# A hybrid decoder layer: one group of forms for the query and key blocks, a later turn of the rotary tables, later angles for the attention, and a later start of five sums

## Chip, cores and metric

The kernel runs on one core of a Trainium2 chip. The metric is device microseconds of one execution. Engines are named as in the profile: PE is TensorE (matmuls), DVE is VectorE, ACT is ScalarE, POOL is GpSimd, SP is SyncE, which here only issues transfers.

## What is computed

One decoder layer on 256 tokens of 2048 features, in float32: a half feed-forward block, then two token mixers side by side (retention and sliding-window attention), then a second half feed-forward block and a gated embedding, with a layer norm after each. Cut to what matters here:

```
h = layer_norm(alpha * h + 0.5 * swiglu(h, w_ffn1_gu, w_ffn1_down), ...)
rq, rk, rv, rg, aq, ak, av, gate_r, gate_a = split(h @ w_in)
rq = rotary(rq as 8 heads of 128, positions, 128, 10000.0)
rk = rotary(rk as 8 heads of 128, positions, 128, 10000.0) * 128 ** -0.5
ro = head_group_norm(retention_chunkwise(rq, rk, rv as 8 heads of 256))
ret_branch = (silu(rg) * ro) @ w_ret_out
aq, ak = rotary(..., 16 of 64 features, 500000.0)
att_branch = sliding_window_attention_sinks(aq, ak, av, att_sinks) @ w_att_out
h = layer_norm(alpha * h + (sigmoid(gate_r) * ret_branch + sigmoid(gate_a) * att_branch) @ w_mix_out, ...)
h = layer_norm(alpha * h + 0.5 * swiglu(h, w_ffn2_gu, w_ffn2_down), ...)
```

The change lies in the mixers: in what is made for `rq`, `rk` and the rotary tables, and in sums of weights of the second feed-forward block that are made ahead during the mixers.

## The kernel before

**Precision and chunks.** A float32 product is made from two reduced-precision parts: a matrix x becomes hi (x rounded, made by an ACT cast) and lo (x minus hi, made by a DVE subtraction), and PE adds three products, lo·hi, hi·hi and hi·lo (L510 to L512). Weights come in chunks of 128 x 1024 floats (512 KB): SP issues the load into a raw tile (names that begin with r), ACT casts it to the hi tile (h, L162) and DVE makes the lo tile (l, L164). One chunk feeds 12 matmuls of 512 columns. So each chunk costs one ACT cast and one DVE subtraction, and PE's program is a row of chunks.

**Sevens.** In some blocks two chunks are worked off by a scheme with seven products instead of eight. It needs sums of weights (tiles u, v and b) and four sums of the activations, called forms. `forms_step(g, step)` makes those of the feature group g: step 0 adds hi and lo to full values (`whole`, tile gaf, L612) and makes the four sums (`forms_sums`, tile sums, L588 to L591), step 1 casts and subtracts (`forms_split`, tiles gafh and gafl). A unit p of a block reads the forms of group p // 2. The query and key blocks (`QK_UNITS`, tiles named rq and rk) use sevens for p = 0 and p = 1.

**Order.** It is written out by hand. The Python program emits for each chunk of PE the making of a chunk about four further on, then the chunk's matmuls, then one step of side work (`run_side`): one entry of the list `side`, one step of the first generator in `slow`, and one of the first in `lazy`. Each engine works its own instructions off in that order and waits where it needs another's result.

**The stage of the change**, in order of PE's time: two blocks of values side by side (tiles rv, 16 chunks), the query block rq, the key block rk, two more blocks of values (rv, eight chunks each), four gate blocks of eight chunks (tiles rg), a block av of four chunks, and then the attention's own products (aqk). What stands beside them:

- `rotary_table("r")` and `rotary_table("a")` make cosines and sines for the retention (tiles posr, rotr, trigr) and for the attention (posa, rota, triga). They are steps of one generator, `angles`, in `slow`. The first step issues the load of the positions on ACT's queue (L990). The second converts them and makes first angles (L993 to L1003), the third to sixth hold the seven rows of the reduction (L1006), then come, a step each, L1010, a sine on ACT (L1012), L1014 to L1018, and a second sine on ACT (L1020).
- `wide_tables` turns the finished retention table by four PE transposes (L1378, tile rtab) and ACT copies it out (L1382, tiles rtabc and rtabs).
- The side jobs of the queries and keys multiply by the wide tables (L1393, L1398, L1401), copy for the transposing transfer (ACT L227, tile wrk), issue it (SP L231, tile mrk), and join its result (ACT L238, tile rk1t).
- The retention of head h: PE makes scores (L1476, tile rs), DVE weighs them with the decay (L1480, L1481, tile rsc), one step later ACT and DVE split them (L113, L114, tile rsp), and one step after that PE multiplies them with the values (L1501, tile ro). Then DVE takes the statistics (L1508, L1509), a Newton root in small operations, and normalizes (L1522). For each pair of heads DVE multiplies by the gate (L1530, tile ron), ACT copies (L227, tile wro), SP issues a transposing transfer (tile mro), ACT joins it (L238), and ACT and DVE make the parts of the result (L1549, L1550, tile rett).
- `sums_ahead(items, wait, every)` in `lazy` makes the sums of weights of ten pairs of chunks of the second feed-forward block and stores them in DRAM. It loads its first pair, lets `wait` steps pass, and then works in four parts with `every` steps between them: two additions (L372, L373, tile u), a cast and two additions (L375 to L377, tile v), a cast and a subtraction (L379, L382, tile lu), a subtraction (L384, tile lv), with the stores (L386, L389) on SP.

Of the kernel before, what the change touches and what calls it, by code (L numbers as in the profile page):

```python
# [70 lines left out]
def layer(ctx: ExitStack, tc: tile.TileContext, io):  # L71
# [281 lines left out]
    def sums_ahead(items, wait, every):  # L353


        def pause():
            for _ in range(every):
                yield

        pairs = [[Chunk(k) for k in items[0]]]  # L360
        for _ in range(wait):
            yield
        for j, (key, _) in enumerate(items):
            a, b = pairs.pop()
            b11, b21, b12, b22 = a.of(a.raw, 0), a.of(a.raw, 1), b.of(b.raw, 0), b.of(b.raw, 1)
            u, v = (slot([P, 2, 512], F32, w + a.name) for w in "uv")
            t1, t3, t2, t4 = (x.rearrange("p (g n) -> p g n", g=2) for x in (u[:, 0], u[:, 1], v[:, 0], v[:, 1]))
            parts = [slot([P, 2, 512], F32R, w + a.name) for w in ("hu", "lu", "hv", "lv")]
            uh, ul, vh, vl = parts
            away = [dram.tile([P, 2, 512], F32, name=f"{w}{a.name}") for w in ("hud", "lud", "hvd", "lvd")]  # L370
            put_by_sums[key] = away
            dve.tensor_tensor(t1, b11, b12, ALU.add)  # L372
            dve.tensor_tensor(t3, b12, b22, ALU.add)  # L373
            yield from pause()
            act.copy(uh, u)  # L375
            dve.tensor_tensor(t2, b11, t3, ALU.add)
            dve.tensor_tensor(t4, t2, b21, ALU.add)  # L377
            yield from pause()
            act.copy(vh, v)  # L379
            if j + 1 < len(items):  # L380
                pairs.append([Chunk(k) for k in items[j + 1]])
            dve.tensor_tensor(ul, u, uh, ALU.subtract)  # L382
            yield from pause()
            dve.tensor_tensor(vl, v, vh, ALU.subtract)  # L384
            for e in range(2):
                sync.dma_start(away[e], parts[e].bitcast(F32))  # L386
            yield from pause()
            for e in range(2, 4):
                sync.dma_start(away[e], parts[e].bitcast(F32))  # L389
# [596 lines left out]
    def rotary_table(nm):  # L986

        inv, sgn = (0, 2) if nm == "r" else (1, 3)
        pos_i = slot([P, S], I32, "pos_i" + nm)
        act.dma_start(pos_i, io["positions"].broadcast_to([P, S]))  # L990
        pos = slot([P, S], F32, "pos" + nm)
        yield
        dve.tensor_copy(pos, pos_i)  # L993
        table = slot([P, 2, S], F32, "trig" + nm)
        cos, sin = trig[nm] = table[:, 0, :], table[:, 1, :]
        w = slot([P, 4, S], F32, "rot" + nm)
        ang, n, na, nb = (w[:, j, :] for j in range(4))
        dve.tensor_scalar(ang, pos, cst[:, inv : inv + 1], None, ALU.mult)
        dve.tensor_scalar(n, ang, INV_2PI, MAGIC, ALU.mult, ALU.add)
        dve.tensor_scalar(n, n, MAGIC, None, ALU.subtract)  # L1000
        dve.tensor_scalar(na, n, 1.0 / 2048.0, MAGIC, ALU.mult, ALU.add)
        dve.tensor_scalar(na, na, MAGIC, 2048.0, ALU.subtract, ALU.mult)
        dve.tensor_tensor(nb, n, na, ALU.subtract)  # L1003
        yield
        for who, j in ((na, 0), (nb, 0), (na, 1), (nb, 1), (na, 2), (nb, 2), (na, 3)):
            dve.scalar_tensor_tensor(ang, who, -TWO_PI[j], ang, ALU.mult, ALU.add)  # L1006
            if who is nb:
                yield
        yield
        dve.tensor_scalar(n, ang, 3.1415925, -3.1415925, ALU.min, ALU.max)  # L1010
        yield
        act.activation(nb, n, AF.Sin)  # L1012
        yield
        dve.tensor_scalar(sin, nb, cst[:, sgn : sgn + 1], None, ALU.mult)  # L1014
        dve.tensor_scalar(na, ang, 1.5707963267948966, None, ALU.add)
        dve.tensor_scalar(n, na, 3.141592653589793, -6.283185307179586, ALU.is_gt, ALU.mult)
        dve.tensor_tensor(na, na, n, ALU.add)
        dve.tensor_scalar(na, na, 3.1415925, -3.1415925, ALU.min, ALU.max)  # L1018
        yield
        act.activation(cos, na, AF.Sin)  # L1020
        yield
# [321 lines left out]
    def mixers(ht, norm, residual, keepers, away):  # L1343
# [29 lines left out]
        def wide_tables():  # L1373
            cos, sin = trig["r"]
            ps = bank("rtab").rearrange("p (w t n) -> p w t n", w=2, t=2)
            for j, v in enumerate((cos, sin)):
                for t in range(2):
                    pe.transpose(ps[:, j, t], v[:, t * P : t * P + P], ident)  # L1378
# [51 lines left out]

        def angles():
            yield from rotary_table("r")
            wide_tables()
            yield
            while len(rk) < 2:
                yield
            yield from rotary_table("a")

        slow.append(angles())
        for p in range(FRONT_PAIRS, KD // 2):  # L1440
            for n in range(2):
# [8 lines left out]
        slots_for_weights(14)  # L1450
        ahead = [(gu_keys("f2", j)(0, p), gu_keys("f2", j)(1, p)) for j in AHEAD for p in AHEAD[j]]
        lazy.append(sums_ahead(ahead[:2], 3, 3))
        lazy.append(sums_ahead(ahead[2:7], 2, 2))
        for b in range(2):
            got = mixer_block("rqk"[0] + "qk"[b], QK_UNITS[b], qk_keys(b), rhs)
            jobs = [rotated(v, f"r{'qk'[b]}{n}", (rq, rk)[b]) for n, v in enumerate(got)]
            assert not side
            side.extend(jobs[0][:3] + [jobs[0][3], jobs[1][0], jobs[0][4], jobs[1][1], jobs[1][2], jobs[1][3], jobs[1][4], jobs[0][6], idle, jobs[1][6]])
        made.clear()
        grp = 8  # L1460
        decay = [slot([P, 2, 384], F32, f"dec{j}") for j in range(4)]
# [648 lines left out]
```

## Time and profile before

| what | us |
|---|---|
| median of 3 runs | 2237.03 (2236.41 to 2239.07) |
| the profiled execution, own time | 2234.48 |
| the profiled execution, span | 2232.6 |
| stretch 750 to 820 of the span (queries and keys), by 10 us: DVE busy | 98 to 100% |
| stretches 820 to 830 and 830 to 840 | 83% and 70% |
| stretch 860 to 870: DVE busy | 57% |
| stretch 900 to 910: DVE busy | 99.6% |
| the same stretch: ACT busy, DMA engines busy | 79%, 75% |

The times of rows in the timeline count from the start of the span. A row gives the start, the time the instruction took, the engine, the line, the operation, its output and inputs, its size and, in brackets, how long the engine stood idle before it and what ended that. The time from the start of one matmul to the start of the next is shorter than what a row gives for it, since matmuls overlap; so costs on PE are read from starts. The same holds for DVE, where the next row starts some 0.08 us before the one ahead of it is noted as ended.

### The profile page before, as it was taken

How to read it: one execution, taken by the hardware profiler on the slowest of the kernel's cores; microseconds unless marked ns; L12 is line 12 of the kernel's file. 1: busy time of each engine (PE TensorE's matmuls, PEld its weight loads, DVE VectorE, ACT ScalarE, POOL GpSimd, SP SyncE). 2: the span in 40 equal slices, each digit the busy share in tenths (PEclk: the TensorE clock that was granted, in tenths of full speed). 3: DMA queues.
4: the chain of work that ended last, by engine and by line, in shares of the span. 5: the costliest groups of instructions: out<-in, count | busy, mean ns of one | idle time of the engine just before them, and what ended most of it. 6: DMA issues, size and time to landing. Idle time of an engine off the chain costs nothing.

```text
span 2232.6 us, 28924 instructions
## 1 busy us (share of the span) xinstructions
PE 2213.7 (99%) x9980; PEld 1827.5 (82%) x9980; DVE 2032.5 (91%) x2666; ACT 1475.6 (66%) x1707; POOL 48.4 (2%) x62
## 2 busy tenths in 40 slices
PE   9999999999999999999999999999999999999998
PEld 8888888888888787888788888888888878888877
DVE  6999999999988998989999888779999999899877
ACT  6877778777564656557866567457767678765553
POOL 0000000000000000000000000000000000000000
PEclk9999999999999999999999999999999999999999
DMA  9979889976687689866986578887899899777771
GB/s 314 274 227 267 248 245 264 246 241 232 231 291 243 234 273 352 277 228 222 286 247 208 185 210 324 321 301 256 294 306 314 290 264 270 218 238 240 279 289 70
DMA packets 315754, 576.00 MB, mean 258 GB/s; under 512 B 107084, under 2 KB 112076, under 8 KB 315608
## 3 DMA queue, kind: packets, MB, share of 16 engines
q1 hardware_dynamic: 305992, 543.79, 73.0%
q0 software_dynamic: 7632, 27.79, 6.6%
q10 hardware_dynamic: 1984, 2.58, 0.3%
q8 instruction: 78, 1.28, 0.2%
q14 instruction: 68, 0.56, 0.1%
HBM read 490.20 MB, written 33.55 MB: 235 GB/s over the span
## 4 chain that ended last, share of the span: by engine, by line
PE 89%; DVE 4%; DMA 4%; ACT 2%; issue 1%; SPq 0%; ACTq 0%; POOL 0%; DVEq 0%; POOLq 0%
PE f2g L512 2%; PE f2g L511 2%; PE f2g L510 2%; PE f1g L510 2%; PE f1g L512 2%; PE f1g L511 2%; PE f2u L512 2%; PE f1u L512 2%; PE f1u L510 2%; PE f1u L511 2%; PE f2u L511 2%; PE f2u L510 2%; PE aqk L461 2%; DMA rf_gu<-in_f_gu 2%; PE f2d L512 1%; PE f1e L511 1%
## 5 line engine op out<-in xcount | busy, mean ns | idle before, releaser
L164 DVE TENSOR_TENSOR lw_in_f<-rw_in_f,hw_in_f 128x1024 fp32r<-128x1024 f32 x124 | 148.7, 1219 | 17.3 <-ACT hw_in_f L162 17.2
L164 DVE TENSOR_TENSOR lf_gu<-rf_gu,hf_gu 128x1024 fp32r<-128x1024 f32 x123 | 145.5, 1222 | 18.6 <-ACT hf_gu L162 17.7
L162 ACT CAST hf_gu<-rf_gu 128x1024 fp32r<-128x1024 f32 x123 | 123.6, 1049 | 26.3 <-DMA rf_gu<-in_f_gu 25.0
L293 ACT CAST hvf_gu<-vf_gu 128x1024 fp32r<-128x1024 f32 x83 | 87.5, 1054 | 76.2 <-DVE vf_gu L289 64.7
L284 ACT CAST huf_gu<-uf_gu 128x1024 fp32r<-128x1024 f32 x83 | 87.3, 1051 | 75.9 <-DVE uf_gu L280 67.7
L164 DVE TENSOR_TENSOR lf_down<-rf_down,hf_down 128x1024 fp32r<-128x1024 f32 x96 | 115.8, 1221 | 22.1 <-ACT hf_down L162 17.4
L162 ACT CAST hw_in_f<-rw_in_f 128x1024 fp32r<-128x1024 f32 x124 | 125.4, 1048 | 6.1 <-DMA rw_in_f<-in_w_in_f 3.9
L162 ACT CAST hf_down<-rf_down 128x1024 fp32r<-128x1024 f32 x96 | 98.4, 1049 | 28.6 <-DMA rf_down<-in_f_down 13.5
L298 DVE TENSOR_TENSOR lvf_gu<-vf_gu,hvf_gu 128x1024 fp32r<-128x1024 f32 x83 | 101.4, 1222 | 0.0
L296 DVE TENSOR_TENSOR luf_gu<-uf_gu,huf_gu 128x1024 fp32r<-128x1024 f32 x83 | 101.4, 1221 | 0.0
L287 DVE TENSOR_TENSOR lf_gu<-rf_gu,hf_gu 128x1024 fp32r<-128x1024 f32 x83 | 101.4, 1221 | 0.0
L277 ACT CAST hf_gu<-rf_gu 128x1024 fp32r<-128x1024 f32 x83 | 86.8, 1046 | 9.5 <-DMA rf_gu<-in_f_gu 9.4
L510 PE MATMUL f1g<-hf_gu,xt 128*128 128x512 f32 x223 | 87.2, 391 | 0.0
L511 PE MATMUL f1g<-hf_gu,xt 128*128 128x512 f32 x223 | 87.0, 390 | 0.0
L512 PE MATMUL f1g<-lf_gu,xt 128*128 128x512 f32 x223 | 87.0, 390 | 0.0
L510 PE MATMUL f2g<-hf_gu,ht 128*128 128x512 f32 x196 | 76.4, 390 | 0.0
L512 PE MATMUL f2g<-lf_gu,ht 128*128 128x512 f32 x196 | 76.3, 389 | 0.0
L511 PE MATMUL f2g<-hf_gu,ht 128*128 128x512 f32 x196 | 76.2, 389 | 0.0
L510 PE MATMUL f1u<-hf_gu,xt 128*128 128x512 f32 x180 | 70.0, 389 | 0.0
L511 PE MATMUL f1u<-hf_gu,xt 128*128 128x512 f32 x180 | 70.0, 389 | 0.0
L512 PE MATMUL f1u<-lf_gu,xt 128*128 128x512 f32 x180 | 70.0, 389 | 0.0
L182 POOL DMA_DIRECT2D lf_gu<-rf_gu x37 | 32.2, 871 | 1641.5 <-DMA rf_gu<-in_f_gu 1134.4
(1640 smaller groups left out, 7331.3 us busy)
## 6 DMA issues: line engine op xcount, KB each, us to landing
rf_gu<-in_f_gu SPq DMA_DIRECT2D x362, 512.0 KB
rf_down<-in_f_down SPq DMA_DIRECT2D x176, 512.0 KB
rw_in_f<-in_w_in_f SPq DMA_DIRECT2D x148, 512.0 KB
lf_gu<-rf_gu POOLq DMA_DIRECT2D x37, 512.0 KB, 8.6
rw_rv<-in_w_rv SPq DMA_DIRECT2D x32, 512.0 KB
rw_ret<-in_w_ret SPq DMA_DIRECT2D x32, 512.0 KB
rw_mix<-in_w_mix SPq DMA_DIRECT2D x32, 512.0 KB
rw_pg<-in_w_pg SPq DMA_DIRECT2D x32, 512.0 KB
```

Of the source, the lines that this page charges most:

```text
L162: act.copy(c.hi, c.raw)
L164: dve.tensor_tensor(c.lo, c.raw, c.hi, ALU.subtract)
L277: act.copy(a.hi, a.raw)
L284: act.copy(uh, u)
L287: dve.tensor_tensor(a.lo, a.raw, a.hi, ALU.subtract)
L293: act.copy(vh, v)
L296: dve.tensor_tensor(ul, u, uh, ALU.subtract)
L298: dve.tensor_tensor(vl, v, vh, ALU.subtract)
L461: pe.matmul(ps[f], hi[:, kk, f * P : (f + 1) * P], rhs(k), start=k == 0, stop=k == n_k - 1,)
L510: pe.matmul(o, al, bh, start=first, stop=False)
L511: pe.matmul(o, ah, bh, start=False, stop=False)
L512: pe.matmul(o, ah, bl, start=False, stop=self.left == 0)
```

## The change

Four edits. The forms of the values' second half: group 1 is made no longer, and group 0 is made one unit later (p = 5 instead of 4). `wide_tables` runs two steps later. The attention's table begins eleven steps after the second key tile is joined, instead of at once; that join itself comes one step later, by a second idle step in the side list. The second group of sums (five items) waits 12 steps instead of 2.

```
@@ def angles():
             yield from rotary_table("r")
+            yield
+            yield
             wide_tables()
-            yield
             while len(rk) < 2:
+                yield
+            for _ in range(11):
                 yield
             yield from rotary_table("a")
@@ for p in range(FRONT_PAIRS, KD // 2):
             for n in range(2):
-                if p in (4, 5):
-                    forms_step(p - 4, n)
+                if p == 5:
+                    forms_step(0, n)
@@
-        lazy.append(sums_ahead(ahead[2:7], 2, 2))
+        lazy.append(sums_ahead(ahead[2:7], 12, 2))
@@ the list of side jobs after each of the two blocks
-            side.extend(jobs[0][:3] + [..., jobs[1][4], jobs[0][6], idle, jobs[1][6]])
+            side.extend(jobs[0][:3] + [..., jobs[1][4], jobs[0][6], idle, idle, jobs[1][6]])
```

**First place, DVE near the end of the first two blocks of values.** The last two chunks there are rv_0_7 and rv_1_7; gaf0 and gaf1 are the forms' groups 0 and 1, rotr is the retention's table. Before:

```order
L1006 SCALAR_TENSOR_TENSOR rotr_6358<-rotr_6358 128x256 x2
L114 TENSOR_TENSOR gaf0l_6389<-sums_6367,gaf0h_6388 128x1024
L1006 SCALAR_TENSOR_TENSOR rotr_6358<-rotr_6358 128x256 x2
L612 TENSOR_TENSOR gaf1w_6408<-ht0_5993 128x1024
L588 TENSOR_TENSOR sums_6410<-gaf1w_6408 128x256
L589 TENSOR_TENSOR sums_6410<-gaf1w_6408 128x256
L590 TENSOR_TENSOR sums_6410<-sums_6410,gaf1w_6408 128x256
L591 TENSOR_TENSOR sums_6410<-gaf1w_6408,sums_6410 128x256
L164 TENSOR_TENSOR lw_rv_0_7_6428<-rw_rv_0_7_6204,hw_rv_0_7_6427 128x1024
L1006 SCALAR_TENSOR_TENSOR rotr_6358<-rotr_6358 128x256 x2
L114 TENSOR_TENSOR gaf1l_6436<-sums_6410,gaf1h_6435 128x1024
L164 TENSOR_TENSOR lw_rv_1_7_6452<-rw_rv_1_7_6224,hw_rv_1_7_6451 128x1024
```

The same place after the change, from the end of the table's first angles on:

```order
L1006 SCALAR_TENSOR_TENSOR rotr_6358<-rotr_6358 128x256 x4
L612 TENSOR_TENSOR gaf0w_6397<-ht0_5993 128x1024
L588 TENSOR_TENSOR sums_6399<-gaf0w_6397 128x256
L589 TENSOR_TENSOR sums_6399<-gaf0w_6397 128x256
L590 TENSOR_TENSOR sums_6399<-sums_6399,gaf0w_6397 128x256
L591 TENSOR_TENSOR sums_6399<-gaf0w_6397,sums_6399 128x256
L164 TENSOR_TENSOR lw_rv_0_7_6417<-rw_rv_0_7_6204,hw_rv_0_7_6416 128x1024
L1006 SCALAR_TENSOR_TENSOR rotr_6358<-rotr_6358 128x256 x2
L114 TENSOR_TENSOR gaf0l_6425<-sums_6399,gaf0h_6424 128x1024
L164 TENSOR_TENSOR lw_rv_1_7_6441<-rw_rv_1_7_6224,hw_rv_1_7_6440 128x1024
```

Ahead of lw_rv_0_7 stood two whole groups but for the second one's split; now one group's sums stand there, and its split comes behind.

**Second place, DVE ahead of the first head's split**, tile rsp0, in the first gate block (its chunks are in_f2_8_0 to 8_7; rota is the attention's table, the f2_gu tiles are sums made ahead, rvl3 is the values' last block). Before:

```order
L1006 SCALAR_TENSOR_TENSOR rota_7639<-rota_7639 128x256 x2
L114 TENSOR_TENSOR rvl3_7693<-rv30_7493,rvh3_7692 128x512
L114 TENSOR_TENSOR rvl3_7693<-rv31_7494,rvh3_7692 128x512
L164 TENSOR_TENSOR lw_in_f2_8_4_7713<-rw_in_f2_8_4_7608,hw_in_f2_8_4_7712 128x1024
L1480 TENSOR_TENSOR rsc0_7721<-rs0_7718,dec0_7293 128x256
L1481 TENSOR_TENSOR rsc0_7721<-rs0_7718,dec0_7293 128x128
L1006 SCALAR_TENSOR_TENSOR rota_7639<-rota_7639 128x256 x2
L384 TENSOR_TENSOR lvf2_gu_3_0_4_7567<-vf2_gu_3_0_4_7563,hvf2_gu_3_0_4_7566 128x1024
L164 TENSOR_TENSOR lw_in_f2_8_5_7742<-rw_in_f2_8_5_7635,hw_in_f2_8_5_7741 128x1024
L114 TENSOR_TENSOR rsp0_7747<-rsc0_7721,rsp0_7747 128x384
```

After:

```order
L114 TENSOR_TENSOR rvl3_7634<-rv30_7461,rvh3_7633 128x512
L114 TENSOR_TENSOR rvl3_7634<-rv31_7462,rvh3_7633 128x512
L164 TENSOR_TENSOR lw_in_f2_8_4_7654<-rw_in_f2_8_4_7559,hw_in_f2_8_4_7653 128x1024
L1483 TENSOR_TENSOR rsc0_7662<-rs0_7659,dec0_7282 128x256
L1484 TENSOR_TENSOR rsc0_7662<-rs0_7659,dec0_7282 128x128
L382 TENSOR_TENSOR luf2_gu_2_0_4_7564<-uf2_gu_2_0_4_7561,huf2_gu_2_0_4_7563 128x1024
L164 TENSOR_TENSOR lw_in_f2_8_5_7684<-rw_in_f2_8_5_7589,hw_in_f2_8_5_7683 128x1024
L114 TENSOR_TENSOR rsp0_7689<-rsc0_7662,rsp0_7689 128x384
```

The whole of the attention's table is gone from there, the conversion and six more rows (L993 to L1003), which stood further ahead, too, and so is one item's row of sums.

**Third place, DVE ahead of the third head's split**, tile rsp2, in the second gate block (chunks in_f2_10_0 to 10_7, then the third block's 12_0 on). Before:

```order
L1550 SCALAR_TENSOR_TENSOR rett1_8098<-ron0t_8090,gn_79,rett1_8098 128x256 x2
L376 TENSOR_TENSOR vf2_gu_4_0_4_8043<-rf2_gu_4_0_4_7949,uf2_gu_4_0_4_8042 128x512
L377 TENSOR_TENSOR vf2_gu_4_0_4_8043<-vf2_gu_4_0_4_8043,rf2_gu_4_0_4_7949 128x512
L164 TENSOR_TENSOR lw_in_f2_12_1_8119<-rw_in_f2_12_1_8015,hw_in_f2_12_1_8118 128x1024
L1480 TENSOR_TENSOR rsc2_8127<-rs2_8124,dec1_7294 128x256
L1481 TENSOR_TENSOR rsc2_8127<-rs2_8124,dec1_7294 128x128
L164 TENSOR_TENSOR lw_in_f2_12_2_8143<-rw_in_f2_12_2_8036,hw_in_f2_12_2_8142 128x1024
L114 TENSOR_TENSOR rsp2_8148<-rsc2_8127,rsp2_8148 128x384
```

After:

```order
L1553 SCALAR_TENSOR_TENSOR rett1_8036<-ron0t_8028,gn_79,rett1_8036 128x256 x2
L1006 SCALAR_TENSOR_TENSOR rota_7958<-rota_7958 128x256 x2
L372 TENSOR_TENSOR uf2_gu_3_0_5_8045<-rf2_gu_3_0_5_7930,rf2_gu_3_1_5_7932 128x512
L373 TENSOR_TENSOR uf2_gu_3_0_5_8045<-rf2_gu_3_1_5_7932 128x512
L164 TENSOR_TENSOR lw_in_f2_12_1_8070<-rw_in_f2_12_1_7951,hw_in_f2_12_1_8069 128x1024
L1483 TENSOR_TENSOR rsc2_8078<-rs2_8075,dec1_7283 128x256
L1484 TENSOR_TENSOR rsc2_8078<-rs2_8075,dec1_7283 128x128
L1006 SCALAR_TENSOR_TENSOR rota_7958<-rota_7958 128x256
L164 TENSOR_TENSOR lw_in_f2_12_2_8095<-rw_in_f2_12_2_7981,hw_in_f2_12_2_8094 128x1024
L114 TENSOR_TENSOR rsp2_8100<-rsc2_8078,rsp2_8100 128x384
```

Here the attention's table has come in; its rows from the conversion to the fourth L1006 stand in the block just ahead (behind the chunk 10_5). In both blocks the sums made ahead are those of an item earlier in the list than before. On ACT the load of the positions has moved with them: it stands behind the cast of chunk 10_4 instead of behind the join of rk1t. PE's own rows stay in their order but for the four transposes rtab, which now stand behind three chunks of the query block instead of one.

More of the change, by code (lines that the diff above doesn't have):

```diff
@@ L1457, in mixers @@
             assert not side
-            side.extend(jobs[0][:3] + [jobs[0][3], jobs[1][0], jobs[0][4], jobs[1][1], jobs[1][2], jobs[1][3], jobs[1][4], jobs[0][6], idle, jobs[1][6]])
+            side.extend(jobs[0][:3] + [jobs[0][3], jobs[1][0], jobs[0][4], jobs[1][1], jobs[1][2], jobs[1][3], jobs[1][4], jobs[0][6], idle, idle, jobs[1][6]])
         made.clear()
```

## Prediction

> **What bounds the kernel now.** I read the page first, then PE's waits, then PE's timeline around the long ones.
>
> ```profile
> span 2232.6 us, 28924 instructions
> PE 2213.7 (99%) x9980; PEld 1827.5 (82%) x9980; DVE 2032.5 (91%) x2666; ACT 1475.6 (66%) x1707; POOL 48.4 (2%) x62
> PE ro L1501 <- DVE rsp L114: 6.0, 2, 5.2
> PE rv L512 <- DVE lw_rv L164: 1.9, 1, 1.9
> PE rtab L1378 <- ACT trigr L1020: 1.1, 1, 1.1
> ```
>
> PE is the bound, and the kernel gets shorter only where PE stands still or runs slowly. The three waits (total, times, longest) all lie in the stage that the change touches. PE's timeline gives their true price, since rows there start .23 us apart when nothing is in the way:
>
> ```profile
> 732.05 0.39 PE L511 MATMUL rv<-hw_rv,ht 128*128 128x512 f32 x1
> 734.38 0.50 PE L512 MATMUL rv<-lw_rv,ht 128*128 128x512 f32 x1 [1.94 <-DVE lw_rv L164]
> 878.73 0.39 PE L511 MATMUL rg<-hw_in_f,ht 128*128 128x512 f32 x1
> 878.95 0.39 PE L512 MATMUL rg<-lw_in_f,ht 128*128 128x512 f32 x1
> 884.54 0.80 PE L1501 MATMUL ro<-rvh,rsp 128*128 128x256 f32 x2 [5.20 <-DVE rsp L114]
> 891.24 0.40 PE L1501 MATMUL ro<-rvh,rsp 128*128 128x256 f32 x2
> 926.34 0.40 PE L1501 MATMUL ro<-rvh,rsp 128*128 128x256 f32 x2
> 930.16 0.40 PE L1501 MATMUL ro<-rvh,rsp 128*128 128x256 f32 x2
> 958.08 0.50 PE L1501 MATMUL ro<-rvh,rsp 128*128 128x256 f32 x2 [0.82 <-DVE rsp L114]
> 989.51 0.40 PE L1501 MATMUL ro<-rvh,rsp 128*128 128x256 f32 x2
> 884.50:891.30 6.80, 6.76 (x22) 5.76 (x23) 6.59 (x18) 4.50 (x6) 0.00 (x0) 0.55 1.01 393
> ```
>
> The ro rows are heads 0, 1, 2, 3, 4 and 6; I write ro0, rs0, rsp0 for head 0. The wait at 734 costs 734.38 - 732.05 - .23 = 2.10. The turn of the tables costs its 1.1. The wait for ro0 costs 884.54 - 878.95 - .23 = 5.36, and more behind it: from ro0 to ro1 PE took 6.70, from ro2 to ro3 for the same work 3.82, so 2.88 went to a slow spell, in which the granted clock was 0.55 (the last row is one of the windows by stretches: busy times, then the granted clock, the DMA engines' share and GB/s). Together 11.4 us stand open.
>
> **The forms.** DVE is late at 734:
>
> ```profile
> 724.38 1.22 DVE L612 TENSOR_TENSOR gaf0w<-ht 128x1024 f32<-128x1024 f32 x1
> 730.31 1.22 DVE L612 TENSOR_TENSOR gaf1w<-ht 128x1024 f32<-128x1024 f32 x1
> 733.11 1.22 DVE L164 TENSOR_TENSOR lw_rv<-rw_rv,hw_rv 128x1024 fp32r<-128x1024 f32 x1
> 735.03 1.22 DVE L114 TENSOR_TENSOR gaf1l<-sums,gaf1h 128x1024 fp32r<-128x1024 f32 x1
> 736.17 1.22 DVE L164 TENSOR_TENSOR lw_rv<-rw_rv,hw_rv 128x1024 fp32r<-128x1024 f32 x1
> ```
>
> A group's sums take 733.11 - 730.31 = 2.80, two L1006 take .80 (874.14 to 874.94, below), a split or a lw 1.14. After the change four L1006 and one group's sums stand ahead of lw_rv_0_7: 724.38 + 1.6 + 2.80 = 728.8, ready at 729.9, where PE wants it at 732.3. The second, behind .80, 1.14 and 1.14, is ready at 733.0 and wanted 2.7 later than the first. Both have 2 us to spare: 2.10 gained; with it go 4.0 us of DVE and a cast on ACT. PE's transposes of the table move two chunks, or 24 starts of .23 = 5.4, later and DVE is 4 us earlier: 1.1 gained, and the table's first use is a block away. If none of this held, 0.
>
> **The angles away from ro0.** DVE's rows there:
>
> ```profile
> 869.07 1.23 DVE L164 TENSOR_TENSOR lw_in_f<-rw_in_f,hw_in_f 128x1024 fp32r<-128x1024 f32 x1 [3.83 <-ACT hw_in_f L162]
> 870.63 0.29 DVE L993 CAST posa<-pos_ia 128x256 f32<-128x256 int32 x1 [0.34 <-DMA pos_ia<-in_positions]
> 873.01 1.22 DVE L164 TENSOR_TENSOR lw_in_f<-rw_in_f,hw_in_f 128x1024 fp32r<-128x1024 f32 x1
> 874.14 0.88 DVE L1006 SCALAR_TENSOR_TENSOR rota<-rota 128x256 f32<-128x256 f32 x2
> 874.94 1.22 DVE L382 TENSOR_TENSOR luf_gu<-uf_gu,huf_gu 128x1024 fp32r<-128x1024 f32 x1
> 872.38 0.59 PE L1476 MATMUL rs<-rq0t,rk0t 128*128 128x256 f32 x2
> 880.34 0.42 DVE L1480 TENSOR_TENSOR rsc<-rs,dec 128x256 f32<-128x256 f32 x1
> 883.93 0.55 DVE L114 TENSOR_TENSOR rsp<-rsc,rsp 128x384 fp32r<-128x384 f32 x1
> 864.62 1.36 ACT L238 COPY rk1t<-mrk 128x1024 uint16<-128x1024 uint16 x1 [2.15 <-DMA mrk<-wrk]
> 864.73 0.34 ACTq L990 DMA_DIRECT2D pos_ia<-in_positions  x1
> ```
>
> rs0 was there at 873.1 and DVE came to it at 880.34, 7.2 late. Ahead of it stood 3.83 of waiting for a cast that sat on ACT behind the join rk1t, .34 for the positions, 2.38 of first angles, 1.6 of L1006 and 1.1 of sums: 9.3, all of which goes (the join comes a step later, behind one more cast, and its transfer no later). From rsc to rsp0 3.59 less .80 remain, so rsp0 comes near 876, with PE wanting ro0 at 879.2. The 5.36 and the 2.88 go.
>
> **Where it comes back.** The table now falls into the second and third gate blocks, where DVE has little room:
>
> ```profile
> 886.87 0.43 DVE L1508 BATCH_NORM_STATS2 gst<-ro 128x6 f32<-128x256 f32 x1
> 907.04 1.22 DVE L1530 TENSOR_TENSOR ron<-ron,rgs 128x1024 f32<-128x1024 f32 x1
> 911.27 1.23 DVE L164 TENSOR_TENSOR lw_in_f<-rw_in_f,hw_in_f 128x1024 fp32r<-128x1024 f32 x1 [0.74 <-ACT hw_in_f L162]
> 918.02 1.69 DVE L1550 SCALAR_TENSOR_TENSOR rett<-ron0t,gn,rett 128x256 fp32r<-128x256 f32 x4 [2.05 <-ACT rett L1549]
> 941.29 0.68 DVE L372 TENSOR_TENSOR uf_gu<-rf_gu,rf_gu 128x512 f32<-128x512 f32 x1
> 957.48 0.55 DVE L114 TENSOR_TENSOR rsp<-rsc,rsp 128x384 fp32r<-128x384 f32 x1
> 988.26 0.55 DVE L114 TENSOR_TENSOR rsp<-rsc,rsp 128x384 fp32r<-128x384 f32 x1
> ```
>
> From ro0's statistics (886.87) to the end of the second gate product (941.29) DVE took 54.4, of which .74 + 2.05 = 2.8 were waits: 51.6 of work. The order leaves as many rows of sums in this piece, and adds the table's first 2.38 and seven L1006 (2.8), 5.2 in all; the rest of the table was in it already. So 56.8, and the two waits are swallowed. It can begin at 880.3 (ro0 at 879.2 and its nine matmuls of 256 columns, half a start of .23 each) and ends at 937.1. Then come copy, transfer, join, and the split of head 4, 16.2 as before (941.29 to 957.48), and PE's start .6 behind it: ro4 at 953.9. PE without waits wants it at 879.2 + 3.82 + 35.10 + 30.92 = 949.0 (ro0 to ro1 at full clock, to ro2, to ro4 less its .82). So ro4 comes 4.9 late instead of .82: **4.1 given back**. ro2 itself is met within half a microsecond by the same sum.
>
> The load of the positions is a wait that DVE has not paid: 864.73 to 870.63 is 5.9 us. It stands now on ACT behind the gate's activation, about 12 us behind ro1 (883.0) by the row below, and a cast, so at 897.1; it lands near 903.0, and DVE is there at 880.3 + 20.2 - 1.8 + 3.4 = 902.1 (907.04 less 886.87, less the 1.8 of table that stood in that piece, plus L1530, one sum, one lw). Between 0 and .9, with no row nearer to either end, I take **.5**. Behind the waiting row stand lw rows that PE needs only four chunks on, and rsp2.
>
> ```profile
> 903.44 1.08 ACT L1569 ACTIVATE rgs<-rg 128x512 f32<-128x512 f32 x2
> ```
>
> Head 6: rsp4 to rsp6 was 30.78, ro4 to ro6 31.43, .65 in hand. The items of sums now run later, so a lv and a lu come in (1.14 each), the lu at a place where DVE waits a little for ACT, but with a cast more on ACT too: between 1.14 - .65 and 2.28 - .65, and I take **1.4**. Each item's two loads and four stores of 512 KB go with it, past the weights' loads on SP; before, too, they ran beside those, and PE waited for no load, so I count nothing (the fourth rival is its price if that fails). Sum: -11.4 + 4.1 + .5 + 1.4 = **-5.4**. The profiled execution (2234.48 with 1.9 outside its span) becomes 2229.1; the median shown is 2.55 above it, so 2231.6. Ends: nothing given back, -11.4; every wait in the gate blocks paid as it stands and the positions in full, near -2.
>
> **The clock.** The wait of 1.94 brought no slow spell, that of 5.20 did. The one I expect at ro4, 4 to 5, lies between. [...]
>
> **Rivals.**
> - **Nothing comes back** (.15). DVE makes good the 5.2 in pauses that I count as fixed (the 2 us waits for rett recur in each block). Then -11.4: 2225.6.
> - **A second slow spell** (.17) behind ro4: +2.88, while head 6 then has time and its 1.4 goes. -3.9: 2233.1. For it speaks the 0.55 after 5.20.
> - **The edit does not free ro0** (.10): rsp0 is held by the weights' casts, as by the 3.83, and not by the table. Then only 2.10 + 1.1 go, and the table's 5.2 less 2.8 of waits, .5 and 1.4 are added: +1.1, 2238.1. Against it: 9.3 of removed rows for 7.2 of lateness.
> - **Slower: stores on SP hold the weights** (.08). SP is in order, and a store of sums that waits for DVE holds the loads behind it:
>
> ```profile
> 882.91 0.34 SPq L389 DMA_DIRECT2D lvdf_gu<-lvf_gu  x1
> ```
>
> Late DVE would make late loads, late casts and later DVE. Two such rounds of 3.83 (869.07), each with a slow spell of 2.88, are 13.4 on top of -5.4: +8, 2245. It decides once DVE lags by the four chunks that are made ahead, 48 starts or 10.9 us. I count on 5.
>
> **Numbers.** The forecast, 2229 to 2234, has .50. A measurement here tells about 0.2%, 4.5 us, from no change: faster means below 2232.5, slower above 2241.5. Faster: .36 of the forecast's .50, the .15, and .05 of the second spell, .56. Same: .14, .12 and .10, .36. Slower: .08. For 8 in 10 the range goes from the full gain to just past the third rival, 2225 to 2238.5.
>
> **What would show it.** Right: no PE wait at rv_0_7, rtab and ro0, a full clock behind ro0, DVE without a gap from ro0's statistics to the first rett, a wait of 4 to 5 us at ro4 and one near 1.4 at ro6. Wrong: ro4's wait under 1 (DVE had more room), a wait still at ro0, or posa with a long wait of its own.

## The result and the profile after

The changed kernel takes 2228.58 us (median of 7 runs, 2227.58 to 2231.04) against 2236.86 (7 runs, 2234.91 to 2239.07) before: a ratio of 0.9965, 95% interval 0.9953 to 0.9976, so faster by 5.4 to 10.5 us. The forecast was 2231.6 in a range of 2225 to 2238.5. The profiled execution took 2227.58, with a span of 2225.5.

PE's waits in the profile after (total, times, longest); the changed kernel has three lines more, so L1501 has become L1504, L1476 L1479 and so on:

```profile
span 2225.5 us, 28896 instructions
PE 2210.3 (99%) x9980; PEld 1826.6 (82%) x9980; DVE 2027.8 (91%) x2660; ACT 1473.8 (66%) x1706; POOL 48.3 (2%) x62
PE ro L1504 <- DVE rsp L114: 5.4, 2, 5.1
...
PE f2u L512 <- DMA lf_gu<-rf_gu: 1.2, 1, 1.2
```

The waits at rv_0_7 and at the table's turn are gone. A long wait for a head's split is still there, of the same length as before, but at ro4 instead of ro0. PE's timeline of after, with the rows between cut: the first value row, rs0, the row ahead of ro4, ro4, ro5, and ro6:

```profile
692.11 0.40 PE L510 MATMUL rv<-hw_rv,ht 128*128 128x512 f32 x1
...
868.49 0.59 PE L1479 MATMUL rs<-rq0t,rk0t 128*128 128x256 f32 x2
...
944.87 0.39 PE L512 MATMUL rg<-lw_in_f,ht 128*128 128x512 f32 x1
950.35 0.80 PE L1504 MATMUL ro<-rvh,rsp 128*128 128x256 f32 x2 [5.09 <-DVE rsp L114]
...
955.56 0.40 PE L1504 MATMUL ro<-rvh,rsp 128*128 128x256 f32 x2
...
983.54 0.51 PE L1504 MATMUL ro<-rvh,rsp 128*128 128x256 f32 x2 [0.32 <-DVE rsp L114]
```

and the windows over ro0's neighbourhood and over ro4's restart (busy time of PE, granted clock, DMA share, GB/s):

```profile
879.00:890.00 11.00, 11.00 (x55) 1.00 0.97 355
950.30:953.30 3.00, 2.95 (x12) 0.51 1.05 404
953.30:960.00 6.70, 6.70 (x35) 1.00 1.02 414
```

The clock behind ro0, 0.55 before, is 1.00 there now; it is 0.51 for three microseconds behind ro4. Laid out from the first row of the values to ro6, with the first rows of before (691.94) and after (692.11) as zero, the stage takes:

| piece | before | after | |
|---|---|---|---|
| first value row to rs0 | 180.44 | 176.38 | -4.06: the waits at rv_0_7 and rtab |
| rs0 to ro0 | 12.16 | 6.79 | -5.37: the wait at ro0 |
| ro0 to ro1 | 6.70 | 3.82 | -2.88: the slow clock |
| ro1 to ro4 | 66.84 | 71.25 | +4.41: the wait at ro4 |
| ro4 to ro5 | 3.92 | 5.21 | +1.29: slow clock behind ro4 |
| ro5 to ro6 | 27.51 | 27.98 | +0.47: ro6 |
| sum | 297.57 | 291.43 | -6.14 |

The spans differ by 7.1. The 0.96 beyond the stage's 6.14 lie ahead of the first value row (+0.17), where nothing was changed, and behind ro6 (-1.13), where only the end of the later sums falls. I take them for scatter: over all the kernels profiled here, the first value row comes at 691.4 to 694.5 and the rest behind ro6 takes 1241.6 to 1244.3.

DVE's rows of after, at the places that the prediction named, with the rows between cut:

```profile
728.99 1.22 DVE L164 TENSOR_TENSOR lw_rv<-rw_rv,hw_rv 128x1024 fp32r<-128x1024 f32 x1
...
869.34 0.42 DVE L1483 TENSOR_TENSOR rsc<-rs,dec 128x256 f32<-128x256 f32 x1 [0.58 <-PE rs L1480]
...
872.14 0.55 DVE L114 TENSOR_TENSOR rsp<-rsc,rsp 128x384 fp32r<-128x384 f32 x1
...
876.56 0.43 DVE L1511 BATCH_NORM_STATS2 gst<-ro 128x6 f32<-128x256 f32 x1 [1.60 <-PE ro L1504]
...
898.35 0.28 DVE L993 CAST posa<-pos_ia 128x256 f32<-128x256 int32 x1
...
906.92 1.66 DVE L1553 SCALAR_TENSOR_TENSOR rett<-ron0t,gn,rett 128x256 fp32r<-128x256 f32 x4
...
931.78 1.22 DVE L1533 TENSOR_TENSOR ron<-ron,rgs 128x1024 f32<-128x1024 f32 x1
...
949.75 0.55 DVE L114 TENSOR_TENSOR rsp<-rsc,rsp 128x384 fp32r<-128x384 f32 x1
```

DVE now waits for rs0 (0.58) and for ro0 (1.60) where it had been 7.2 late; the positions are there when posa is made (898.35, no bracket), the first rett waits for nothing; and rsp4 starts at 949.75, 0.6 ahead of the ro4 that stood for it.

### The profile page after: what moved, and what is told of

Read it like the earlier page. It is cut to its first block, busy times and chain, and to the rows that moved or that the text cites. A ratio compares the mean times of both kernels' runs of the same rounds, so it can differ in the third digit from the quotient of the medians.

```text
span 2225.5 us, 28896 instructions
## 1 busy us (share of the span) xinstructions
PE 2210.3 (99%) x9980; PEld 1826.6 (82%) x9980; DVE 2027.8 (91%) x2660; ACT 1473.8 (66%) x1706; POOL 48.3 (2%) x62
## 3 DMA queue, kind: packets, MB, share of 16 engines
q8 instruction: 78, 1.28, 0.2%
## 4 chain that ended last, share of the span: by engine, by line
PE 87%; DVE 5%; DMA 4%; ACT 2%; issue 2%; SPq 0%; ACTq 0%; DVEq 0%; POOLq 0%
PE f2g L510 2%; PE f2g L511 2%; PE f2g L512 2%; PE f1g L512 2%; PE f1g L511 2%; PE f1g L510 2%; PE f1u L511 2%; PE f1u L512 2%; PE f1u L510 2%; PE f2u L512 2%; PE f2u L510 2%; PE f2u L511 2%; PE aqk L461 2%; PE f1d L511 1%; PE f1e L510 1%
## 5 line engine op out<-in xcount | busy, mean ns | idle before, releaser
L164 DVE TENSOR_TENSOR lw_in_f<-rw_in_f,hw_in_f 128x1024 fp32r<-128x1024 f32 x124 | 148.6, 1218 | 10.3 <-ACT hw_in_f L162 9.5
```

What stands on the lines that cost most here:

```text
L164: dve.tensor_tensor(c.lo, c.raw, c.hi, ALU.subtract)
```

## The experiments

Two measures are taken from each trace in the same way. **D** is the start of rsp0 on DVE less the start of rs0 on PE: before 883.93 - 872.38 = 11.55, after 872.14 - 868.49 = 3.65. A ro0 that waits for nothing comes 6.79 behind rs0 (after), and ro0 starts 0.61 behind the start of rsp0 (884.54 - 883.93), so **the wait at ro0 should be D - 6.18**. The **stage** is the length from the first value row to ro6, as in the table above. Waits are excess between starts, as in the prediction. "Before" is the kernel before, run beside each kernel on the same chip. The three "_only" kernels and rq0 shared one chip; after_again, ang_back, sums_back and sums_4 a second; forms_back, idle_back, rq0_e3 and rq0_e3b a third. D, the waits and the stage are read from one profiled execution of each kernel.

| kernel | median us (runs) | before | difference | D | wait at ro0, ro2, ro4 | stage |
|---|---|---|---|---|---|---|
| before | | | | 11.55 | 5.36, 0, 0.98 | 297.57 |
| forms_only | 2230.39 (10) | 2235.44 | -5.0 | 12.95 | 6.75, 0, 3.02 | 297.70 |
| ang_only | 2233.84 (10) | 2235.44 | -1.6 | 8.91 | 2.70, 1.08, 4.92 | 299.58 |
| sums_only | 2231.14 (10) | 2235.44 | -4.3 | 6.41 | 0.2, 0.59, 3.48 | 294.62 |
| sums_4 | 2235.56 (10) | 2236.07 | -0.5 | 10.21 | 4.01, 0, 2.80 | 297.32 |
| after_again | 2228.56 (6) | 2236.07 | -7.5 | 3.66 | 0, 0, 5.20 | 291.41 |
| forms_back | 2231.60 (10) | 2236.05 | -4.4 | 3.66 | 0, 0, 5.21 | 293.97 |
| sums_back | 2231.93 (10) | 2236.07 | -4.1 | 7.95 | 1.75, 1.10, 4.61 | 293.27 |
| ang_back | 2228.65 (5) | 2236.07 | -7.4 | 6.50 | 0.31, 2.22, 2.59 | 292.96 |
| idle_back | 2229.12 (5) | 2236.05 | -6.9 | 3.66 | 0, 0.26, 4.70 | 291.16 |
| rq0 | 2223.84 (5) | 2235.44 | -11.6 | 4.17 | 0, 0, 0.95 | 287.01 |
| rq0_e3 | 2224.84 (5) | 2236.05 | -11.2 | 3.85 | 0, 0, 0 | 286.31 |
| rq0_e3b | 2224.67 (4) | 2236.05 | -11.4 | 3.15 | 0, 0, 0.92 | 286.68 |

D - 6.18 gives the measured wait at ro0 within 0.03 in the six kernels with a wait in brackets at ro0. So the question of what freed ro0 is the question of what shortened D.

**One edit alone, on the kernel before.** First the forms.

```
-                if p in (4, 5):
-                    forms_step(p - 4, n)
+                if p == 5:
+                    forms_step(0, n)
```

> The kernel before with the first edit alone (one group of forms, one unit later). My theory: the wait at rv_0_7 (2.10 in the trace of before) and the one at the table's turn (1.1) go, and nothing of the rest changes, since VectorE is paced by TensorE and by loads behind the key block: ro0 still waits 5.2 and has its slow spell. 2236.9 - 3.2 = 2233.7, between 2233 and 2235. Rival: VectorE's work ahead of rsp0 stands at fixed times behind a load, so what TensorE gains is waited for at ro0: its wait grows to about 8 and the time is 2236 to 2237.

The ratio was 0.9979 (0.9970 to 0.9988), 2.7 to 6.7 us. The waits at rv_0_7 and rtab are gone although the turn of the tables stands at its old place. PE's timeline at ro0 and ro4:

```profile
882.61 0.79 PE L1501 MATMUL ro<-rvh,rsp 128*128 128x256 f32 x2 [6.60 <-DVE rsp L114]
...
957.34 0.51 PE L1501 MATMUL ro<-rvh,rsp 128*128 128x256 f32 x2 [2.86 <-DVE rsp L114]
```

rs0 comes 4.05 earlier (176.39 in place of 180.44), and rsp0 only 2.65, so D grew by 1.4 and ro0 waits 6.75. That is the rival's sign, at about half of the size it gave, and with 3.02 at ro4 the profiled execution gained nothing in the stage. The median of 2230.39 lies below what either theory gave (2233 to 2235, and 2236 to 2237). The profiled execution was the second slowest of ten, at 2234.09; where the others gained is not shown, since they left no trace. In the traced one nothing freed ro0.

The table alone:

```
             while len(rk) < 2:
                 yield
+            for _ in range(11):
+                yield
             yield from rotary_table("a")
```

> The kernel before with the attention's table alone moved eleven steps later. By the rows of before, the table's rows and the positions ahead of rsp0 are worth 0.34 + 0.29 + 2.1 + 1.6 = 4.3 to 4.6. My theory, that each row ahead of rsp0 counts and the 3.83 wait for a cast is a separate share which this edit does not remove: ro0 waits 5.36 - 4.5 = about 0.8 without a slow spell, the 3.83 stays, ro4 waits about 5 and ro6 a little: -8.24 + 0.8 + 4.4 + 1 = -2, so 2234.9, between 2233.5 and 2236. If the table alone holds ro0, its wait is 0 and the 3.83 shrinks with it: 2234. If the weights' casts alone hold it, ro0 still waits over 4 and ro4 waits too: 2240 to 2242.

Ratio 0.9996 (0.9986 to 1.0005): no gain that can be told from none. The profiled execution was the slowest of ten (2237.98). The keys' last product and the join rk1t, then DVE's weights, then PE:

```profile
854.21 1.22 DVE L1401 TENSOR_TENSOR evz<-evz,rk1x 128x1024 f32<-128x1024 f32 x1
...
866.26 2.56 ACT L238 COPY rk1t<-mrk 128x1024 uint16<-128x1024 uint16 x2 [2.57 <-DMA mrk<-wrk]
...
870.71 2.36 DVE L164 TENSOR_TENSOR lw_in_f<-rw_in_f,hw_in_f 128x1024 fp32r<-128x1024 f32 x2 [4.24 <-ACT hw_in_f L162]
...
875.63 1.23 DVE L164 TENSOR_TENSOR lw_in_f<-rw_in_f,hw_in_f 128x1024 fp32r<-128x1024 f32 x1 [1.43 <-ACT hw_in_f L162]
```

```profile
882.51 0.50 PE L1503 MATMUL ro<-rvh,rsp 128*128 128x256 f32 x2 [2.55 <-DVE rsp L114]
...
958.39 0.79 PE L1503 MATMUL ro<-rvh,rsp 128*128 128x256 f32 x2 [4.76 <-DVE rsp L114]
```

All the table's rows have left, and D fell by only 2.64: DVE, earlier at the weights, waits for their casts, 4.24 and 1.43 where before it was 3.83. From the join to rsp0 it takes 15.65 in place of 19.31, but the join itself comes 1.0 later (866.26 - 692.57 = 173.69 behind the first value row, against 864.62 - 691.94 = 172.68). ro0 keeps 2.70 where my theory had 0.8, and the whole price at ro4 (4.92, and 2.3 of slow clock behind it) is paid.

The sums alone:

```
-        lazy.append(sums_ahead(ahead[2:7], 2, 2))
+        lazy.append(sums_ahead(ahead[2:7], 12, 2))
```

> The kernel before with the five sums alone begun at 12 steps instead of 2. In the trace of before VectorE waits 4.19 us at 841.3 for the load of such a pair, and four rows of sums stand ahead of the keys' last product L1401, which ends 7.8 later than in the trace of after (852.98 against 845.21). Theory of the sums: with this edit alone the join rk1t comes 5 to 8 us earlier and the 3.83 wait for a cast goes; the table's rows stay and now wait for the positions' load (up to 3.8): ro0 waits 2 to 4, ro4 stays at 0.8: 2232 to 2234.5. Theory of my prediction, that the table's rows are what matters and the sums only shift work: ro0 waits 4 or more with a slow spell: 2235.5 to 2237.

Ratio 0.9981 (0.9972 to 0.9990); the median, 2231.14, lies below both theories' ranges. The keys' last product, the join, and DVE around rsp0, then rs0, ro0 and ro4 on PE:

```profile
849.62 1.22 DVE L1401 TENSOR_TENSOR evz<-evz,rk1x 128x1024 f32<-128x1024 f32 x1
...
860.27 1.37 ACT L238 COPY rk1t<-mrk 128x1024 uint16<-128x1024 uint16 x1 [1.18 <-DMA mrk<-wrk]
...
876.20 0.88 DVE L1006 SCALAR_TENSOR_TENSOR rota<-rota 128x256 f32<-128x256 f32 x2
...
879.26 0.55 DVE L114 TENSOR_TENSOR rsp<-rsc,rsp 128x384 fp32r<-128x384 f32 x1
```

```profile
872.85 0.59 PE L1476 MATMUL rs<-rq0t,rk0t 128*128 128x256 f32 x2
...
879.87 0.51 PE L1501 MATMUL ro<-rvh,rsp 128*128 128x256 f32 x2
...
953.84 0.80 PE L1501 MATMUL ro<-rvh,rsp 128*128 128x256 f32 x2 [3.32 <-DVE rsp L114]
```

The table's rows stand where they stood (876.20), and ro0 has no wait in brackets any more. D fell by 5.14 and the slow clock behind ro0 went with the wait. Counted from the first value row (692.42 here, 691.94 before), L1401 comes 3.84 earlier than before and the join 4.83. This is the edit that frees ro0, and it has a price of its own: ro4 waits 3.48.

**The load or the rows?** In the trace of before, DVE stood waiting for a sum's load ahead of the keys' last product, L1401 (rows between cut):

```profile
841.29 0.69 DVE L372 TENSOR_TENSOR uf_gu<-rf_gu,rf_gu 128x512 f32<-128x512 f32 x1 [4.19 <-DMA rf_gu<-in_f_gu]
...
852.98 1.22 DVE L1401 TENSOR_TENSOR evz<-evz,rk1x 128x1024 f32<-128x1024 f32 x1
```

The sums could have held ro0 by that wait or by their rows. Begun at 4 steps, the pair has more time to land while nearly all rows stay:

```
-        lazy.append(sums_ahead(ahead[2:7], 2, 2))
+        lazy.append(sums_ahead(ahead[2:7], 4, 2))
```

> The kernel before with the five sums begun at 4 steps instead of 2, nothing else. Ahead of the keys' last product stand the same rows of the sums but one (L382, 1.1 us), and ahead of rsp0 all but one; only the pair's load has two steps, some 5 us, more. If the load is what mattered: no wait of VectorE for it, L1401 of the keys 4 to 5.5 us earlier, ro0 waits under 1.5 and has no slow spell, ro4 waits 1 to 3: 3.5 to 6 us below the kernel before. If the rows of the sums matter: ro0 still waits over 4 with its spell: within 1.5 us of the kernel before.

Ratio 0.9997 (0.9988 to 1.0007). The profiled execution was the slowest of ten (2236.30). No sum waits for its load in this trace, and ro0 still waits 4.01 (the first value row is at 694.51 here):

```profile
853.25 1.22 DVE L1401 TENSOR_TENSOR evz<-evz,rk1x 128x1024 f32<-128x1024 f32 x1
...
871.68 0.29 DVE L993 CAST posa<-pos_ia 128x256 f32<-128x256 int32 x1 [1.92 <-DMA pos_ia<-in_positions]
...
885.17 0.55 DVE L114 TENSOR_TENSOR rsp<-rsc,rsp 128x384 fp32r<-128x384 f32 x1
```

```profile
885.77 0.50 PE L1501 MATMUL ro<-rvh,rsp 128*128 128x256 f32 x2 [3.85 <-DVE rsp L114]
```

D fell by 1.34 alone. Counted from the first value row, L1401 came 2.30 earlier than before (158.74 in place of 161.04), and 1.14 of that is the row L382, which now stands behind it; so the load's 4.19 was worth about 1.2 there. The rest went into waits for casts. Then DVE stood 1.92 for the positions, where it had been 0.34 before. My theory that the load is the main price falls. The gain goes with the rows: ahead of rsp0 stood two whole sums before the change, 2 x (0.6 + 0.6 + 0.7 + 0.6 + 1.14 + 1.14) = 9.6 us. With 4 steps one row of 1.14 is out of it, and D falls by 1.34. With 12 steps one sum less its last row is left, 3.6, and D falls by 5.14 for 6.0 us of rows. The sums' casts on ACT and their loads and stores move together with these rows, and no run moved them apart; that DVE's rows alone are the price is argued from this count.

**One edit undone, on the kernel after.** after_again is the yardstick.

> The kernel after, once more, as the yardstick on the same chip for the three others: 8 us under the kernel before, with a wait near 5 at ro4 and none at ro0.

It agreed with the first profile in the stage to 0.02. forms_back makes two groups of forms again:

> The kernel after with the first edit undone: two groups of forms again. Theory so far, that VectorE's rows in front of a waiting tile are what counts and that the edits can be taken one by one: the wait of 2.10 at rv_0_7 is back, the one at the table's turn is not (the turn stays two steps later), ro0 keeps its freedom (2.0 us of slack ahead of rsp0, and the keys' chain is late only by what TensorE is late too), ro4 as in after: 2 to 3 us above the kernel after, 2230.5 to 2232. Rival: the 4.0 us of forms on VectorE reach the end of the keys' chain, since VectorE is busy without a gap from 750 to 820: ro0 waits 1 to 3 as well: 4 to 6 us above the kernel after, 2232.5 to 2235.

3.0 above the yardstick; in the stage 2.56, which is the wait at rv_0_7 (2.11, and short ones in restarting). The turn of the tables has no wait, ro0 none. sums_back sets the sums to 2 steps:

> The kernel after with the five sums begun at 2 steps again (all else kept). Theory of the load: VectorE waits 4 us or more near 838 for a sum's load, the join rk1t comes late, the casts behind it too, ro0 waits 1.5 to 4 and ro4 about 5: 2 to 5 us above the kernel after. Theory of my prediction: the table has gone from there, so ro0 is free (wait under 0.5), ro6's 0.5 goes with the sums: within 1 us of the kernel after.

3.4 above the yardstick, as the theory of the load had it, but the theory of the rows has the same here; sums_4 tells the two apart. DVE waits for the load as before, and ro0 waits although the table is elsewhere:

```profile
837.93 0.69 DVE L372 TENSOR_TENSOR uf_gu<-rf_gu,rf_gu 128x512 f32<-128x512 f32 x1 [4.53 <-DMA rf_gu<-in_f_gu]
```

```profile
877.10 0.50 PE L1504 MATMUL ro<-rvh,rsp 128*128 128x256 f32 x2 [1.59 <-DVE rsp L114]
```

ang_back starts the table at once (without the loop of eleven steps):

> The kernel after with the attention's table begun at once again (the eleven steps undone, all else kept). Theory of the load: what held ro0 before was the 4.19 us that VectorE waited for a sum's load at 841, which the later sums have removed, and the table's rows alone do not reach ro0: no wait there over 0.7, and ro4 waits 3.3 as with the later sums alone instead of 5.1, with a shorter slow spell: 1.5 to 3 us below the kernel after, 2225.5 to 2227.5. Theory of my prediction, that the table's rows have to leave ro0: they stand again ahead of rsp0, 4.3 of rows and up to 3.8 for the positions against 2.0 of slack and 2.8 of idle time: ro0 waits 2.5 to 5, ro4 falls to 1: 0 to 4 us above the kernel after.

It is level with the yardstick (0.9966, 0.9953 to 0.9979, against 0.9966, 0.9955 to 0.9978), as far as such intervals tell, some 4 us. ro0 waits 0.31, so the table has no need to leave it; but both theories were off behind it, since ro2 and ro4 wait 2.22 and 2.59, each with a slow spell. idle_back takes the second idle step out:

> The kernel after with the second idle step taken out again, so that the keys' join comes a step earlier and, with it, the start of the attention's table. My prediction gave this step no term of its own; theory of VectorE's queue: the join waits about 2.5 us longer for its transfer on ScalarE (1.12 becomes 2 to 4), which ScalarE's idle 3.19 at 865 takes: within 1 us of the kernel after. Rival: the casts behind the join come late, as they did before the change (3.83), and rsp0 with them: ro0 waits 1 to 3: 2230 to 2232.

0.6 above the yardstick, 0.25 below it in the stage: nothing that can be told from none.

**A better place for the table.** After the change DVE still stands idle in the last two blocks of values, for 5.3 us up to 845. rq0 puts the table there:

```
-            while len(rk) < 2:
+            while len(rq) < 2:
                 yield
-            for _ in range(11):
+            for _ in range(0):
                 yield
             yield from rotary_table("a")
```

> The kernel after, with the attention's table begun as soon as the second query tile is joined, in the last two blocks of values, where VectorE of after stands idle 2.05 + 1.95 + 1.08 + 0.16 up to 845 and 0.68 + 1.97 + 1.81 + 1.99 up to 866. The table is 7.1 us of VectorE. Theory that VectorE's queue sets the waits at ro4 and ro6: both go (5.25 + 1.1 of slow clock + 0.6), L1401 of the keys comes 2 to 2.5 later, the join rk1t waits 3 to 3.5 instead of 1.12, which ScalarE's idle 3.19 at 865 takes, and ro0 has no wait: 2228.6 - 7 = 2221.7, between 2220.5 and 2223.5. Rival: the keys' chain (product, copy, transfer, join) passes the delay on to the casts and to rsp0, ro0 waits 2 to 5 again: 2224 to 2230. Second rival: something other than VectorE's queue holds rsp4 (the loads of the weights): ro4 waits 3 or more: 2226 to 2228.

Ratio to before 0.9950 (0.9938 to 0.9963), where the change itself has 0.9965: 3.4 us below it by the ratios, whose intervals overlap, 4.7 by the medians, 4.4 in the stage. All five times (2223.15 to 2225.54) lie below all of the change's. ro0 is free, and PE's rows at ro4 and ro6 show what is left:

```profile
946.38 0.50 PE L1504 MATMUL ro<-rvh,rsp 128*128 128x256 f32 x2 [0.80 <-DVE rsp L114]
...
979.58 0.50 PE L1504 MATMUL ro<-rvh,rsp 128*128 128x256 f32 x2 [1.62 <-DVE rsp L114]
```

The table's rows on DVE, 7.1 us in all, had cost 4.3 of wait and 1.3 of slow clock at ro4, and cost PE nothing in the values' blocks; ro6 takes 1.3 of it back (ro5 to ro6 29.28, in after 27.98). I had expected ro4 and ro6 without a wait, and 2220.5 to 2223.5. What holds ro6 can be read from DVE: from rsp4 to rsp6 it takes 33.19 in rq0, 33.18 in after and 33.20 in sums_only, where before it took 30.78. These 2.4 us came with the later sums. The last two kernels therefore spread the sums, begun at 13 and at 15 steps, with every third step in place of every second:

> The kernel with the attention's table in the last two blocks of values (which took 2223.8), with the five sums begun at 13 steps and three steps apart instead of two, so that fewer of their rows stand between the statistics of one pair of heads and the scores of the next. Of sums ahead of rsp4, behind ro2, there are then 1.1 + 2.3 + 0 us instead of 1.1 + 2.3 + 1.4, ahead of rsp6 3.6 + 0 between split and product instead of 3.6 + 1.1. If VectorE's queue sets these waits: ro4 from 0.95 to 0, ro6 from 1.77 to about 1: 1 to 2 us below, 2222 to 2223. If the transfers of the result set them: no change, 2223.8. If the sums, which now end later, are missing in the attention's products: 2225 to 2228.

> The same with the five sums begun at 15 steps, three apart: ahead of rsp4, behind ro2, 1.1 + 1.1 + 1.2 us of sums, ahead of rsp6 2.5 + 1.1 + 1.1. If VectorE's queue sets the waits, and rows ahead of the product count more than those in its shadow: ro4 and ro6 within 0.7 of nothing: 2221.5 to 2223. If the transfers set them: 2223.8.

Neither is faster (2224.84 and 2224.67), where the theory of DVE's queue had 2222 to 2223 and 2221.5 to 2223. The first has no wait at ro4, but PE's waits in its trace name new places:

```profile
PE ro L1504 <- DVE rsp L114: 1.7, 1, 1.7
...
PE as L1605 <- DVE aq L1297: 1.1, 1, 1.1
PE gt L512 <- DVE lw_in_f L164: 0.9, 1, 0.9
```

The sums that left the gate blocks stand in front of the attention's products (L1605). In the second, ro6 is down to 0.5 (ro5 to ro6 takes 27.99, before 27.51) and the wait at gt is the same 0.9.

## Why the prediction held, and where its reason was wrong

- **The forms: right.** lw_rv_0_7 was forecast ready at 729.9 and was made from 728.99 on; the waits at rv_0_7 and rtab went. The gain to rs0 was 4.06 instead of 3.2: the wait at rtab cost 1.23 between starts and not 1.1 (743.80 - 742.34 - 0.23), and behind the two waits five rows of before start 0.33 to 0.42 after the one ahead of them (734.71, 737.44, 737.78, 745.09 and 745.42), 0.6 in all above steps of 0.23. For rtab either of two edits is enough: forms_only has the turn at its old place, forms_back two groups of forms, and neither waits there.
- **ro0: right in size, wrong in cause.** The 5.36 and the 2.88 went, as forecast. The step that failed is "9.3, all of which goes": it set 4.3 us of positions and table and 1.1 of sums against 7.2 of lateness, and put the 3.83 of waiting for a cast down to the join's place. By the runs the table alone is worth 2.64 of D, the sums alone 5.14, the idle step nothing. The 3.83 hangs on the rows of the sums ahead of L1401, which lie 30 us further back than my count went: L1401 came 161.04 after the first value row before, at 157.20 with the sums later, and at 161.64 with the table moved. With the sums later the wait for the cast shrank to 2.06; with the table moved it stayed (4.24). Over all the kernels here the join starts 10.3 to 12.2 behind L1401, whatever the edit, and rsp0 comes 18.2 to 20.2 behind the join with the table between them, 14.7 to 15.7 without it where ro0 still waits. So the path to ro0 runs through L1401 and the join, the sums lengthen it ahead of L1401 and the table behind the join. The sum came out because the change makes both edits at once: that is luck.
- **ro4: right.** 4.9 was forecast, against 5.25 (950.35 - 944.87 - 0.23); what it cost over before, 4.1 against 4.41. DVE had no gap from ro0's statistics to the first rett, as the step said; to the end of the second gate product (L1533, 931.78 + 1.14) it took 56.4, forecast 56.8, and from there to rsp4 16.8, forecast 16.2. That the table's rows made most of it is shown by rq0, where 0.95 is left; that the later sums made a part, by sums_only, where ro4 waits 3.48 with the table at its old place. DVE was near its limit there in any case: forms_only has neither and waits 3.02.
- **The positions: no cost** where I took 0.5, the low end of that term.
- **ro6: 0.47 where I took 1.4.** The slow clock behind ro4 held PE up by 1.3, which gave rsp6 that time; the second rival had said so. rq0 bears it out: with no slow clock at ro4 the same stretch of DVE, 33.2 from rsp4 to rsp6, leaves 1.77 at ro6, and 0.47 + 1.29 is 1.76. The rows that I counted there were right, at the high end.
- **The clock: wrong chance.** I gave a slow spell at ro4 .17, as a rival, and left it out of the sum. That chance was an estimate of mine that no run had shown: before had no spell behind the wait of 1.94 and one behind that of 5.20. It came, at 1.29 instead of 2.88. All nine waits of 4 us or more in these traces were followed by one.
- **Rivals.** "Nothing comes back", "ro0 not freed" and the stores on SP did not happen: the gate blocks gave back 6.17 of 12.31, and PE waits for no load in this stage (the order on SP was as I took it: before, SP waited 3.6 for L384 ahead of the store at 882.91, and the four loads of weights behind that store began to go out at 883.34). "A second slow spell" did, at half its price. The reason given for "ro0 not freed", that the casts hold rsp0 and not the table alone, was half right: with the table alone moved ro0 keeps 2.70.
- **The number.** -5.4 was forecast for the profiled execution and the stage gave -6.14. In that sum the slow clock that I left out (1.29) and the two terms that I took too large (0.93 at ro6, 0.5 for the positions) nearly cancel, which is luck too. 0.96 more lie in the scatter outside the stage. The median of after stands 1.0 above its profiled execution, where I carried over the 2.55 of before. That makes the 3.0 us between 2231.6 and 2228.58.

What the change is worth by parts: undone one at a time, the sums 3.4, the forms 3.0, the idle step 0.6 and the table 0.1, against 7.5 for the whole in after_again. These are differences of medians, the forms and the idle step on another chip than the yardstick, and each is uncertain by some 3 to 4 us; made alone, the forms, the sums and the table gave 5.0, 4.3 and 1.6, which is more than the whole, so the parts do not simply add. The eleven steps of the table, the largest move of the change, bring nothing that these times can tell, and 1.5 in the stage of one trace (292.96 against 291.41).

Still open: how the faster executions of forms_only gained their 5 us while the profiled one gained nothing; whether a sum's rows on DVE or its casts on ACT weigh more ahead of L1401.

## What to carry to other kernels

When an engine that works its rows off in the program's order, as DVE does here (the rows of before from 877.21 to 883.93 stand as they were written), comes late to a row, go back to the last place where it waited for the engine that is the bound, and sum every row from there, also through a wait that a third engine seems to cause: a wait for a cast can be, at least in part, the echo of rows 30 us earlier on the waiting engine itself (here 3.83 shrank to 2.06 with the sums later). When several edits go in together, take each out alone: here the one that moved most was worth nothing that could be told from none. And before work is moved from a full stretch to another, look for the stretch where the engine stands idle: 7.1 us of table cost 5.6 us at ro4 and nothing in the values' blocks, and 4.4 of the stage came back by moving it.

## What the runs showed of the hardware

**Behind some short waits PE ran at half the clock** (granted 0.55, 0.51 and 0.50 in before, after and sums_only; rows of 512 columns 0.43 apart instead of 0.23). Waits at ro0, ro2 and ro4, counted between starts, and the slow time behind them (the span from that head to the next less its 3.82 to 3.92 at full clock), and with them the wait at rv_0_7, which five of the traces have:

| wait | slow time behind it |
|---|---|
| 1.75 (sums_back), 1.10, 1.08, 0.98 | none over 0.1 |
| 2.10 to 2.11 at rv_0_7 (before, ang_only, sums_4, forms_back) | no slow spell |
| 2.10 at rv_0_7 (sums_only) | eight starts 0.43 apart, about 1.6 |
| 2.22, 2.59 (ang_back) | 1.57, 1.36 |
| 2.70 (ang_only), 2.80 (sums_4) | 0.1, 0 |
| 3.02 (forms_only), 3.48 (sums_only) | 1.60, 1.51 |
| 4.01 to 5.36, eight waits | 1.28 to 2.88 |
| 6.75 (forms_only) | 2.03 |

PE's rows in ang_back behind its wait at ro2, with the rows between cut, the windows' row of that stretch, and the windows' row of sums_only behind its wait at rv_0_7 (the granted clock is the number ahead of the last two):

```profile
917.36 0.51 PE L1502 MATMUL ro<-rvh,rsp 128*128 128x256 f32 x2 [2.06 <-DVE rsp L114]
...
917.82 0.61 PE L1502 MATMUL ro<-rvh,rsp 128*128 128x256 f32 x2
...
919.51 0.63 PE L511 MATMUL rg<-hw_in_f,ht 128*128 128x512 f32 x1
919.94 0.63 PE L512 MATMUL rg<-lw_in_f,ht 128*128 128x512 f32 x1
...
921.22 0.41 PE L512 MATMUL rg<-lw_in_f,ht 128*128 128x512 f32 x1
921.47 0.40 PE L510 MATMUL rg<-hw_in_f,ht 128*128 128x512 f32 x1
```

```profile
917.30:923.00 5.70, 5.64 (x23) 0.70 1.05 400
```

```profile
735.50:738.50 3.00, 3.00 (x8) 0.50 0.00 0
```

Rows of 512 columns stand 0.43 apart there (919.51 to 919.94), the slow stretch runs from 917.82 to 921.22, 3.4 us, and from 921.47 on they stand 0.23 apart. In sums_only the spell used up time that PE loses at the table's turn in before, so rs0 comes no later for it (180.43 and 180.44). For an estimate on this kernel the table gives: no spell behind its four waits up to 1.75, one behind five of its eleven from 2.10 to 3.48, and 1.28 to 2.88 of slow time behind each of the nine from 4.01 on. What decides between 2.10 and 3.48 no run shows.
